# A two-layer hybrid decoder trunk on one core: early weight loads for blocked jobs, whole S5 table steps on one engine, memory through DRAM, and a new order of the work

## The chip, the cores and the metric

The kernel runs on one core of a Trainium2 chip. The metric is the device time of one execution in microseconds; of several runs the median is taken. The engines are TensorE (PE in the profile), VectorE (DVE), ScalarE (ACT), GpSimd (POOL) and SyncE (SP), which here issues every DMA.

## The reference, cut to what matters

The input is x of 512 tokens by 1024 channels in float32, 256 memory tokens, and weights for two layers. Each layer computes

```python
h = rms_norm(x, norm_pre)
c = h @ w_in                       # 9668 columns, split among the branches and the merge gates
y0 = rwkv7(c_A)                    # 4 heads, delta-rule state over the tokens
y1 = dsa(c_B, positions)           # an indexer keeps 128 keys per query, attention over these
y2 = retention(c_C, positions)     # chunks of 128 tokens
y3 = s5(c_D)                       # diagonal complex state space model, then a GLU
y4 = cross_attention(c_X, rms_norm(mem, norm_mem) @ w_mem_kv)
m  = sum(sigmoid(gate_i) * (y_i @ w_branch[i]) for i in range(5))
x  = x + rms_norm(m @ w_out, norm_post)
```

and the second layer starts from the x of the first.

## The kernel before, in words

The large products run on TensorE in three passes: each float32 operand is split into a high and a low part (fp32r), and high by high, high by low and low by high are summed. A weight block of 256 KB is loaded by SP into a tile `raw` (five buffers), ScalarE casts it to `wh`, and VectorE forms the rest `wl = raw - wh` (four buffers each). A class `Load` does this; `prefetch(upto)` issues loads up to five blocks ahead of the one in use and splits up to two ahead.

All instructions are issued in an order that the Python program works out while it builds the kernel. It has two kinds of work. **Dense jobs** (`Job`) are products with weights: column groups of w_in by name (`rq`, `rk`, `rv`, `w`, `wg`, `xq`, ...), the memory's keys and values (`mem`, `mem1`), the gates of branch i with its branch projection (`g0` to `g4`), and the output projection of each half of the tokens. `select()` takes the next dense job: the first in the list `ORDER` whose inputs are there and for whose kept result there is room. Room is counted in tiles of the pools c1, c2 and c4 (10, 14 and 16 tiles). A job for which there is no room is not taken, and its weights are not loaded; if none can be taken, `prefetch` has nothing to load.

**Lanes** (`Lane`) are the branches, the tables of S5 (`tab`), the splits of the memory (`ms0`, `ms1`), the start of a layer and its end (`finish_out`). Each is a generator that yields between its steps. At most `MAXL` lanes are active; they are started in the order of `LANES`, each when its inputs are there and there is room (`dsa>0` waits for y0 too, `s5>2` for y2, and so on). `run` takes a step of the first active lane whose last step has ended by the planner's own clocks at least 1 us ago (`EARLY`), unless the planner has VectorE or ScalarE more than `LAG` us behind TensorE; otherwise it issues the next piece of the dense job. So the dense work fills the time between the steps of the branches.

Each engine executes its instructions in the order of issue, and so does SP with the DMAs.

The parts that the change touches: `select` and `dense` (jobs), `s5_tables` (the lane `tab`), `mem_transposed` and `mem_split` (the normalised memory `memT`, two c4 tiles that are held under the owner `mem` until `ms1` is done), `out_jobs` and `finish_out` (the output projection and the sum with x), and the lists `ORDER` and `LANES`. In `s5_tables` a table of powers is built by doubling: for m = 1, 2, 4, ... 64, and for the real and the imaginary part, two products and their sum or difference on 8 x m columns. For each single instruction `any_` asks the planner which of VectorE and GpSimd is free sooner. After the last doubling, SP stores the table to DRAM (`s5tab`).

Of the kernel before, what the change touches and what calls it, by code (L numbers as in the profile page):

```python
# [222 lines left out]
def hybrid_kernel(ctx: ExitStack, tc: tile.TileContext, x, mem, positions, norm_pre, norm_post, norm_mem, w_in,  # L223
# [21 lines left out]
    def sb(name, shape, dt=F32, bufs=2, lane="c", big=False):  # L245
# [5 lines left out]
        if n == 4096 and dt == F32:  # L251
            return bp.tile(list(shape), dt, name=name, tag="mg", bufs=1)
# [204 lines left out]
    def mem_transposed():  # L457
# [118 lines left out]
    class Job:  # L576


        def __init__(self, gen, loads, need=(), done=None, keep=None, frees=(), after=None, merge=None, gate=None):
            self.gen, self.loads, self.need, self.done, self.frees, self.after = gen, loads, need, done, frees, after  # L580
            self.owner, self.room = (keep[0], {keep[1]: keep[2]}) if keep else (None, {})
            self.taken, self.merge, self.gate = False, merge, gate
            jobs.append(self)

    taken, merging, queue, active, opened = [], [], [], [], []

    def select():
# [13 lines left out]
        jb = next((j for j in left if (j.after is None or j.after.taken) and have(j.need) and fits(j, lanes)), None)  # L601
        if jb is None:
# [3 lines left out]
        hold(jb.owner, **jb.room)  # L606
        if last(jb):
            hold("mhl0", c4=4)
# [189 lines left out]

    def mem_split(l):

        h = [sb("mh", [128, 4, NMEM], F32R) for _ in range(2)]
# [602 lines left out]
    def s5_tables(l):  # L1404
# [11 lines left out]
        def any_(n_, name, *a, **kw):  # L1416
            e = V if sched.soonest(dve=n_ / 960, pool=n_ / 450) == "dve" else G
            getattr(e, name)(*a, **kw)
# [4 lines left out]
        while m < 128:  # L1423
# [42 lines left out]
        m_ = m1.rearrange("p b i c -> p i b c")  # L1466
        for i, (a, b) in enumerate(((0, 0), (1, 1), (1, 0), (0, 1))):
            any_(128, "tensor_tensor", m_[:, i], Bt[:, a], f_[b], op=OP.mult)
        any_(128, "tensor_tensor", Bb[:, 0], m_[:, 0], m_[:, 1], op=OP.subtract)
        any_(128, "tensor_tensor", Bb[:, 1], m_[:, 2], m_[:, 3], op=OP.add)  # L1470
        yield

        def outer(dst, coef, mat, neg):

            for r_ in range(2):
                any_(1024, "memset", dst[r_], 0.0)

            def pr(a, b, d):
                any_(512, "tensor_tensor", d, coef[:, a, o, :, None].to_broadcast([128, nb, 4, 16]),
                     mat[:, b, :, None, :].to_broadcast([128, nb, 4, 16]), op=OP.mult)  # L1480
            for r_ in range(2):
# [3 lines left out]
                yield  # L1485
                if neg and r_:
                    any_(512, "tensor_scalar", m1, m1, -1.0, None, op0=OP.mult)
                for q in range(2):
                    h = slice(64 * q, 64 * q + 64)
                    any_(512, "tensor_tensor", dst[r_][h, :, :, q, :], m1[h], m2[h],  # L1490
                         op=OP.add if r_ and not neg else OP.subtract)
# [195 lines left out]
    def out_jobs(l):  # L1687
# [3 lines left out]
        for half in range(2):  # L1691
            lds = {(e, k): Load(wv[:, k:k + 2, 256 * e:256 * e + 256]) for e in range(4) for k in range(0, 8, 2)}

            def gen(half=half, lds=lds):
# [4 lines left out]
                g = ST[l, "npost"]  # L1699
                for e in range(4):  # L1700
                    o = slice(256 * (e % 2), 256 * (e % 2) + 256)
                    for k in range(8):
                        w = lds[e, k - k % 2]
                        if k % 2 == 0:
                            prefetch(w.idx)
                            if k == 2:
                                flush()
                        mh, ml = ST["mhl", l, half, k // 4]
                        for i in range(2):
                            if k == 0 and e % 2 == 0:  # L1710
                                pss[i][e // 2] = psb() if half == 0 or (i == 0 and e == 0) else psd()
                            t = slice(128 * i, 128 * i + 128)
                            p = pss[i][e // 2][:, o]
                            for a, (x_, y_) in enumerate(((mh, w.hi), (mh, w.lo), (ml, w.hi))):
                                T.matmul(p, x_[:, k % 4, t], y_[:, k % 2, :], start=k == 0 and a == 0 and e % 2 == 0,
                                         stop=k == 7 and a == 2 and e % 2 == 1, skip_group_check=True)
# [4 lines left out]
                    if e:  # L1721
                        a, b = (0, 512) if e == 1 else (256 * e, 256)
                        for i in range(2):
                            v = pss[i][a // 512][:, a % 512:a % 512 + b]
                            j = sched.ring("gth", 2, bp.tile([128, S], F32, name="gth", tag="gth", bufs=2))
                            A.activation(j[:, :b], v, AF.Square, scale=1.0 / 32, accum_out=rr[i][:, e - 1:e])
                            V.tensor_tensor(u[i][:, a:a + b], v, g[:, a:a + b], op=OP.mult)
                ST[l, "fin", half] = (u, rr, xi)
# [22 lines left out]
    def dense():  # L1751
        while True:
# [10 lines left out]
            prefetch(jb.loads[0].idx)  # L1763
# [178 lines left out]
```

## Time and profile before

| | |
|---|---|
| median of 3 runs | 1466.64 us (1465.48 to 1467.06) |
| the profiled execution | 1470.27 us, of which its span 1468.5 us |
| TensorE busy | 1394.2 us, 95% of the span, 7774 matmuls |
| VectorE, ScalarE, GpSimd busy | 942.5, 558.0 and 274.2 us |
| mean granted clock of TensorE | 0.971 |
| DMA | 168.51 MB, a mean of 115 GB/s |

The span runs from the first to the last instruction. TensorE's clock has two levels, 2.4 GHz (granted clock 1.0) and 1.2 GHz (0.5); the granted clock of a stretch is a mean over it. All instructions carry line 209, the line of the helper that records them, so that they are told apart by their tiles: `wh`, `wl` and `raw` are weights, `hh` and `hl` the normalised x, `mgs` the merged sum, `sar`, `sta` and `sem` the S5 tables, `dsc` the scores of DSA, `dac` its indexer, `xp` the cross-attention's probabilities, `ors` and `ou` the end of a layer.

### The profile page before, as it was taken

What the parts mean: (1) busy time and instruction counts of PE and PEld (TensorE: products, weight loads), DVE (VectorE), ACT (ScalarE), POOL (GpSimd) and SP (SyncE); (2) the same over time, 40 slices, a digit from 0 to 9 for tenths busy, and PEclk for the clock granted to TensorE, in tenths of its full rate; (3) what the DMA queues carried; (4) which work ended last, traced back from release to release, by engine and by line L of the source; (5) the groups of instructions that cost most, each with busy time, mean ns of one, the idle gap of its engine ahead of it and who ended that gap; (6) DMA issues with size and microseconds to landing.
All of it is one profiled execution on the core that took longest, in us unless ns stands there. A gap on an engine that the chain in (4) does not pass through costs nothing.

```text
span 1468.5 us, 21717 instructions
## 1 busy us (share of the span) xinstructions
PE 1394.2 (95%) x7774; PEld 1160.9 (79%) x7774; DVE 942.5 (64%) x2020; ACT 558.0 (38%) x1196; POOL 274.2 (19%) x336
## 2 busy tenths in 40 slices
PE   5998999999999999989986999999999999999997
PEld 5977678878888978768886987777888878877887
DVE  5776555657765977634664566577888777734555
ACT  4533443333333333333544452433332333243343
POOL 0365230000310121100008533220011101311000
PEclk9999889999999999979998999999999999999999
DMA  6741334355322533313564743234444323423355
GB/s 188 191 122 56 114 108 102 83 169 151 94 65 72 145 89 98 102 35 93 159 194 130 204 119 93 66 100 123 116 129 143 102 68 76 109 64 79 100 159 179
DMA packets 242839, 168.51 MB, mean 115 GB/s; under 512 B 27593, under 2 KB 228267, under 8 KB 242731
## 3 DMA queue, kind: packets, MB, share of 16 engines
q1 hardware_dynamic: 242731, 167.12, 41.1%
q8 instruction: 61, 1.00, 0.3%
q14 instruction: 47, 0.39, 0.1%
HBM read 143.49 MB, written 17.83 MB: 110 GB/s over the span
## 4 chain that ended last, share of the span: by engine, by line
PE 79%; DVE 6%; POOL 5%; DMA 4%; ACT 3%; issue 2%; SPq 1%; DVEq 0%; ACTq 0%; POOLq 0%
PE d L209 60%; PE b L209 19%; POOL sar L209 2%; DMA raw<-in_w_out_dram 1%; DVE wl L209 1%; SPq L209 1%; DMA raw<-in_w_in_dram 1%; POOL sm L209 1%; POOL sta L209 1%; DVE x L209 1%; POOL rsw L209 1%; ACT wh L209 0%; DMA npre<-in_norm_pre_dram 0%; DMA posi<-in_positions_dram 0%; POOL sem L209 0%
## 5 line engine op out<-in xcount | busy, mean ns | idle before, releaser
L209 PE MATMUL d<-hh,wh 128*128 128x512 f32 (+1 forms) x1232 | 489.8, 398 | 13.4 <-ACT wh L209 13.4
L209 PE MATMUL d<-hh,wl 128*128 128x512 f32 (+1 forms) x1232 | 475.6, 386 | 14.2 <-DVE wl L209 14.1
L209 PE MATMUL d<-hl,wh 128*128 128x512 f32 (+1 forms) x1232 | 473.9, 385 | 0.0
L209 DVE TENSOR_TENSOR wl<-raw,wh 128x512 fp32r<-128x512 f32 (+1 forms) x448 | 328.5, 748 | 120.5 <-ACT wh L209 118.5
L209 ACT CAST wh<-raw 128x512 fp32r<-128x512 f32 (+1 forms) x448 | 267.4, 618 | 127.2 <-PE d L209 74.1
L209 PEld LDWEIGHTS d<-hh,wh 128*128 128x128 f32 x1232 | 236.9, 192 | 73.7 <-ACT wh L209 15.6
L209 PEld LDWEIGHTS d<-hh,wl 128*128 128x128 f32 x1232 | 236.2, 192 | 66.4 <-DVE wl L209 18.4
L209 PEld LDWEIGHTS d<-hl,wh 128*128 128x128 f32 x1232 | 236.8, 192 | 42.5 <-issue 0.5
L209 POOL TENSOR_TENSOR mg<-mg,gth 128x512 f32<-128x512 f32 x48 | 67.9, 1415 | 459.7 <-DVE gth L209 459.7
L209 ACT ACTIVATE gth<-d 128x512 f32<-128x512 f32 (+1 forms) x90 | 52.0, 578 | 163.5 <-PE d L209 162.6
L209 DVE SCALAR_TENSOR_TENSOR gth<-gth,d 128x512 f32<-128x512 f32 x64 | 44.0, 687 | 102.9 <-PE d L209 97.5
L209 PE MATMUL b<-wh,mgs 128*128 128x256 f32 x320 | 63.7, 284 | 5.2 <-ACT wh L209 3.8
L209 PE MATMUL d<-yh,wh 128*128 128x512 f32 x160 | 63.3, 395 | 0.0
L209 PE MATMUL d<-yl,wh 128*128 128x512 f32 x160 | 63.2, 395 | 0.0
L209 PE MATMUL d<-yh,wl 128*128 128x512 f32 x160 | 63.2, 395 | 0.0
L209 PEld LDWEIGHTS b<-wh,mgs 128*128 128x128 f32 x320 | 52.2, 191 | 6.1 <-ACT wh L209 4.0
L209 DVE MAX8 dm<-dac 128x8 f32<-128x256 f32 (+2 forms) x96 | 53.0, 552 | 0.1
L209 DVE MATCH_REPLACE8 dac<-dm,dac 128x256 f32<-128x256 f32 (+2 forms) x96 | 52.1, 543 | 0.0
L209 POOL TENSOR_TENSOR ors<-ors,mhalf 128x1 f32<-128x1 f32 x8 | 4.6, 586 | 230.5 <-DVE ors L209 230.5
L209 PE MATMUL b<-wl,mgs 128*128 128x256 f32 x160 | 45.6, 285 | 0.6 <-DVE wl L209 0.6
L209 PE MATMUL d<-wh,mgs 128*128 128x256 f32 x192 | 41.3, 288 | 2.3 <-DVE ou L209 2.3
L209 POOL TENSOR_TENSOR rsw<-rsw,sinT 128x1024 f32<-128x1024 f32 (+1 forms) x12 | 28.9, 2412 | 67.2 <-DMA rsw<-rk 23.7
(397 smaller groups left out, 2084.4 us busy)
## 6 DMA issues: line engine op xcount, KB each, us to landing
raw<-in_w_in_dram SPq DMA_DIRECT2D x324, 256.0 KB, 3.3
raw<-in_w_out_dram SPq DMA_DIRECT2D x64, 256.0 KB, 3.1
raw<-in_w_branch_dram SPq DMA_DIRECT2D x40, 256.0 KB, 3.6
x<-in_x_dram SPq DMA_DIRECT2D x8, 512.0 KB, 6.1
raw<-in_w_mem_kv_dram SPq DMA_DIRECT2D x16, 256.0 KB, 2.7
s5tab<-sar SPq DMA_DIRECT2D x8, 256.0 KB, 2.4
s5Wi<-sar SPq DMA_DIRECT2D x4, 512.0 KB, 2.9
nn<-wNt SPq DMA_DIRECT2D x8, 256.0 KB, 2.1
```

The source lines that it names most:

```text
L209: r = f(*args, **kw)
```

## The change

1. `select` may take a job for which there is no room: it is marked as not granted, its weights are loaded and split as for any job, and `dense` grants it (and only then issues its matmuls) when room has come free. Only one such job is open at a time, and none is taken while an active lane waits for something that is not there.
2. In `s5_tables` each group of instructions that follow from one another (two products and their sum) goes to one engine, chosen once for the group by `free_for`; the clearing of the outer products is always on GpSimd, and there is one more yield after each squaring of the factor.
3. The normalised memory is written to DRAM by the setup, its two tiles are given up after `ms0`, and `ms1` loads them again (and asks for 6 c4 tiles in place of 4).
4. In the last quarter of the output columns of the last two token tiles of layer 1, the two tiles are done one after the other, and the first is finished while the second is computed.
5. `LAG` goes from 7.5 to 11.5, `MAXL` from 4 to 6, and `ORDER` and `LANES` are new.

```diff
-LAG = 7.5
+LAG = 11.5
-MAXL = 4
+MAXL = 6
-ORDER = ("rv w rsg xq xsg ssg g4 g1 wg su mem di g2 dq dsg dk mem1 dv g3 g0",
-         "dv xsg w g3 di rsg su wg ssg g2 g4 dk g0 dq dsg g1")
-LANES = ("rwkv ms0 tab dsa>0 s5 ret ms1>3 x idx", "x ret idx tab s5>2 rwkv dsa")
+ORDER = ("rsg rv w wg g0 xq xsg di su dsg ssg dq g4 g2 dk mem1 dv g3 mem g1",
+         "xsg dq g0 w di rsg wg g4 su dsg ssg dk dv g3 g1 g2")
+LANES = ("ret idx>4 s5>4 ms1>3 rwkv dsa ms0 tab x>2", "idx>4 dsa>0 tab ret x rwkv>t s5")
...
+        for k in range(2):
+            SY.dma_start(memd[k], memT[k])
...
-        jb = next((j for j in left if (j.after is None or j.after.taken) and have(j.need) and fits(j, lanes)), None)
-        if jb is None:
+        if any(not t.granted for t in begun):
+            return False
+        able = [j for j in left if (j.after is None or j.after.taken) and have(j.need)
+                and not (opened and j.gate is not None and j.gate[1] == 0)]
+        jb = next((j for j in able if fits(j, lanes)), None)
+        if jb is None and able:
+            jb = able[0]
+            if last(jb) or not all(have(q.need) for q in active):
+                return False
+            jb.granted = False
+        elif jb is None:
             jb = left[0]
             if not fits(jb, lanes) and (active or not fits(jb)):
                 return False
...
             for r_ in range(2):
-                any_(nb * m, "tensor_tensor", d[r_], a[0], e[r_], op=OP.mult)
-                any_(nb * m, "tensor_tensor", t, a[1], e[1 - r_], op=OP.mult)
-                any_(nb * m, "tensor_tensor", d[r_], d[r_], t, op=OP.add if r_ else OP.subtract)
+                en = free_for(3 * nb * m)
+                en.tensor_tensor(d[r_], a[0], e[r_], op=OP.mult)
+                en.tensor_tensor(t, a[1], e[1 - r_], op=OP.mult)
+                en.tensor_tensor(d[r_], d[r_], t, op=OP.add if r_ else OP.subtract)
                 yield
             m *= 2
             if m < 128:
                 cmul(G, em2, em, em, ea, eb)
                 em, em2 = em2, em
+                yield
...
+                    if e == 3 and half and l == L - 1:
+                        for i in range(2):
+                            for k in range(8):
+                                if i == 0 and k % 2 == 0:
+                                    prefetch(lds[e, k].idx)
+                                products(e, k, i)
+                                if k % 2:
+                                    yield
+                            evict(e, i)
+                            if i == 0:
+                                flag(f"out{l}1a")
+                        continue
...
             prefetch(jb.loads[0].idx)
+            while not jb.granted:
+                if room_for({"c4": 6} if jb.last else jb.room):
+                    grant(jb)
+                else:
+                    yield 1e9
...
-                    "ms1": Lane(lambda: mem_split(1), ("ms0",), "ms1", c4=4),
+                    "ms1": Lane(lambda: mem_split(1), ("ms0",), "ms1", c4=6),
```

## Rows read from the trace of the kernel before

**Rows 1.** The page's first part: busy time, share of the span, instructions.
```profile
PE 1394.2 (95%) x7774; PEld 1160.9 (79%) x7774; DVE 942.5 (64%) x2020; ACT 558.0 (38%) x1196; POOL 274.2 (19%) x336
```

**Rows 2.** Windows: stretch, length, each engine's busy time, granted clock, DMA share, GB/s.
```profile
0.00:45.00 45.00, 28.70 (x190) 26.67 (x191) 27.41 (x61) 23.63 (x43) 2.51 (x10) 0.96 0.64 183
...
103.00:245.00 142.00, 130.29 (x717) 105.51 (x717) 82.58 (x188) 59.70 (x148) 43.10 (x43) 0.90 0.36 102
245.00:620.00 375.00, 373.67 (x1977) 304.46 (x1976) 261.05 (x560) 126.14 (x253) 48.86 (x37) 1.00 0.39 104
620.00:670.00 50.00, 44.13 (x210) 35.47 (x209) 15.56 (x38) 17.61 (x41) 2.78 (x2) 0.80 0.24 64
...
735.00:905.00 170.00, 147.64 (x1057) 136.28 (x1056) 100.49 (x185) 75.68 (x184) 73.75 (x115) 0.93 0.54 155
905.00:1421.00 516.00, 513.28 (x2651) 413.39 (x2651) 346.16 (x746) 182.30 (x367) 66.37 (x55) 1.00 0.37 100
1421.00:1469.00 48.00, 37.10 (x306) 36.09 (x304) 29.22 (x59) 20.77 (x54) 2.28 (x4) 0.94 0.53 172
```

**Rows 3.** Waits of TensorE over the span: total us, times, longest us.
```profile
PE d L209 <- DVE wl L209: 15.4, 7, 11.3
PE d L209 <- ACT wh L209: 13.4, 7, 6.2
```

**Rows 4.** Timeline of VectorE, 793 to 812 us: start, length, instruction, idle before it.
```profile
807.99 0.69 DVE L209 TENSOR_TENSOR sar<-sar,sta 128x512 f32<-128x512 f32 x1 [13.63 <-POOL sta L209]
808.60 2.49 DVE L209 TENSOR_TENSOR wl<-raw,wh 128x512 fp32r<-128x512 f32 x4
```

**Rows 5.** Timeline of GpSimd, 797 to 810 us.
```profile
806.91 1.04 POOL L209 TENSOR_TENSOR sta<-sar,sem 128x512 f32<-128x512 f32 x1
```

**Rows 6.** Windows around the stall in the S5 tables of layer 1.
```profile
797.70:809.30 11.60, 0.33 (x3) 0.12 (x2) 1.31 (x3) 1.62 (x3) 10.02 (x18) 0.63 0.12 46
809.30:814.50 5.20, 5.16 (x24) 5.16 (x25) 1.79 (x3) 0.06 (x1) 0.78 (x3) 0.50 0.65 146
814.50:822.00 7.50, 7.35 (x61) 7.11 (x61) 4.09 (x4) 4.50 (x10) 7.42 (x10) 1.00 1.06 269
```

**Rows 7.** Waits of the DMA queue, 784 to 822 us: total, times, longest.
```profile
SPq L209 <- POOL sar L209: 11.8, 1, 11.8
```

**Rows 8.** Timeline of the DMA queue, 793 to 813 us.
```profile
805.98 3.52 SPq L209 DMA_DIRECT2D s5tab<-sar  x4
...
812.40 0.57 SPq L209 DMA_DIRECT2D raw<-in_w_in_dram  x1
```

**Rows 9.** Tile wl, 784 to 890 us: ns min/median/max, first and last start.
```profile
L209 DVE TENSOR_TENSOR wl<-raw,wh x35: 678/693/1784, 784.1 to 885.9; 128x512 fp32r<-128x512 f32 x35
```

**Rows 10.** Timeline of the DMA queue, 125 to 150 us.
```profile
134.71 9.07 SPq L209 DMA_DIRECT2D kv<-gth  x2
...
145.07 2.94 SPq L209 DMA_DIRECT2D raw<-in_w_in_dram  x5
```

**Rows 11.** Windows of 10 us.
```profile
190.00:200.00 10.00, 8.72 (x60) 7.59 (x59) 6.20 (x10) 4.81 (x15) 9.05 (x10) 0.83 0.01 2
200.00:210.00 10.00, 8.34 (x43) 6.50 (x45) 2.80 (x7) 4.13 (x16) 1.78 (x2) 0.50 0.92 273
```

**Rows 12.** Tile xp in layer 0: ns min/median/max, first and last start, forms.
```profile
L209 ACT ACTIVATE xp<-b,xmx x16: 464/473/480, 193.4 to 230.8; 128x256 f32<-128x256 f32 x16
```

**Rows 13.** Tile dac in layer 0.
```profile
L209 DVE TENSOR_SCALAR dac<-b,diw x3: 478/618/750, 403.2 to 540.6; 128x256 f32<-128x256 f32 x1, 128x384 f32<-128x384 f32 x1, 128x512 f32<-128x512 f32 x1
```

**Rows 14.** Tile dsc in layer 0.
```profile
L209 ACT ACTIVATE dsc<-dsc,dmx x16: 386/556/721, 530.5 to 643.6; 128x128 f32<-128x128 f32 x4, 128x256 f32<-128x256 f32 x4, 128x384 f32<-128x384 f32 x4, 128x512 f32<-128x512 f32 x4
```

**Rows 15.** Timeline of the end, 1459.9 to 1469 us.
```profile
1460.79 0.38 ACT L209 ACTIVATE gth<-d 128x256 f32<-128x256 f32 x1
...
1462.12 1.06 POOL L209 TENSOR_TENSOR ors<-ors,mhalf 128x1 f32<-128x1 f32 x2 [22.85 <-DVE ors L209]
1462.70 2.74 DVE L209 SCALAR_TENSOR_TENSOR x<-ou,ors,x 128x512 f32<-128x512 f32 x4 [0.46 <-POOL ors L209]
```

More of the change, by code (lines that the diff above doesn't have):

```diff
@@ L251, in sb @@
         if n == 4096 and dt == F32:
-            return bp.tile(list(shape), dt, name=name, tag="mg", bufs=1)
+            return sched.ring("mg", 1, bp.tile(list(shape), dt, name=name, tag="mg", bufs=1))
         c, w = next((c, w) for c, w in ((1, 256), (2, 516), (4, 1032), (16, 4096)) if n <= w and not (big and c == 1))
@@ L581, in __init__, with grant @@
             self.owner, self.room = (keep[0], {keep[1]: keep[2]}) if keep else (None, {})
-            self.taken, self.merge, self.gate = False, merge, gate
+            self.taken, self.merge, self.gate, self.granted = False, merge, gate, True
             jobs.append(self)
-    taken, merging, queue, active, opened = [], [], [], [], []
+    taken, merging, queue, active, opened, begun = [], [], [], [], [], []
+    def grant(jb):
+        hold(jb.owner, **jb.room)
+        if jb.last:
+            hold("mhl0", c4=4)
+        jb.granted = True
     def select():
@@ L605, in select @@
                 return False
-        hold(jb.owner, **jb.room)
-        if last(jb):
-            hold("mhl0", c4=4)
+        jb.last = last(jb)
+        begun[:] = [t for t in begun if not t.granted] + [jb]
+        if jb.granted:
+            grant(jb)
         if jb.merge is not None:
@@ L796, in to_fm @@
         return ps
+    memd = dp.tile([2, 128, 4, NMEM], F32, name="memd")
     def mem_split(l):
+        if l:
+            memT[:] = [sb("memT", [128, 4, NMEM]) for _ in range(2)]
+            for k in range(2):
+                SY.dma_start(memT[k], memd[k])
+            yield
         h = [sb("mh", [128, 4, NMEM], F32R) for _ in range(2)]
@@ L1485, in outer @@
                 yield
+                en = free_for(1024)
                 if neg and r_:
[L1487 removed]
+                    en.tensor_scalar(m1, m1, -1.0, None, op0=OP.mult)
                 for q in range(2):
                     h = slice(64 * q, 64 * q + 64)
[L1490 to L1491 removed]
+                    en.tensor_tensor(dst[r_][h, :, :, q, :], m1[h], m2[h], op=OP.add if r_ and not neg else OP.subtract)
                     yield
@@ L1699, in gen, with products @@
                 g = ST[l, "npost"]
-                for e in range(4):
-                    o = slice(256 * (e % 2), 256 * (e % 2) + 256)
+                ST[l, "fin", half] = (u, rr, xi)
+                def products(e, k, i):
+                    mh, ml = ST["mhl", l, half, k // 4]
+                    w = lds[e, k - k % 2]
+                    o = slice(256 * (e % 2), 256 * (e % 2) + 256)
+                    if k == 0 and e % 2 == 0:
+                        pss[i][e // 2] = psb() if half == 0 or (i == 0 and e == 0) else psd()
+                    t = slice(128 * i, 128 * i + 128)
+                    p = pss[i][e // 2][:, o]
+                    for a, (x_, y_) in enumerate(((mh, w.hi), (mh, w.lo), (ml, w.hi))):
+                        T.matmul(p, x_[:, k % 4, t], y_[:, k % 2, :], start=k == 0 and a == 0 and e % 2 == 0,
+                                 stop=k == 7 and a == 2 and e % 2 == 1, skip_group_check=True)
@@ L1702, in gen @@
                     for k in range(8):
-                        w = lds[e, k - k % 2]
                         if k % 2 == 0:
-                            prefetch(w.idx)
+                            prefetch(lds[e, k].idx)
                             if k == 2:
                                 flush()
-                        mh, ml = ST["mhl", l, half, k // 4]
                         for i in range(2):
[L1710 to L1716, printed above, removed]
+                            products(e, k, i)
@@ L1721, in gen @@
                     if e:
-                        a, b = (0, 512) if e == 1 else (256 * e, 256)
                         for i in range(2):
[L1724 to L1728, printed above, removed]
+                            evict(e, i)
             after = Job(gen, list(lds.values()), done=f"out{l}{half}", need=tuple(f"merged{l}{i}" for i in range(5)),
@@ L1828, in run @@
                     hold("memkv" + pick.name[2], c4=4)
-                    if pick.name == f"ms{L - 1}":
-                        release("mem")
+                    release("mem")
                 if pick.name[0] == "y":
@@ L1906, in hybrid_kernel @@
         for i in range(4):
-            lanes += [Lane(lambda l=l, i=i: finish_out(l, i), (f"out{l}{i // 2}",), f"t{l + 1}{i}", c4=1)]
+            lanes += [Lane(lambda l=l, i=i: finish_out(l, i), (f"out{l}1a" if l == L - 1 and i == 2 else f"out{l}{i // 2}",),
+                           f"t{l + 1}{i}", c4=1)]
     run(lanes)
```

26 lines of the change are left out of this document (17 added, 9 removed).

## The prediction

> **What bounds the kernel now.** I read the page's busy times first: TensorE is busy for 1394.2 of 1468.5 us, far ahead of VectorE with 942.5 [rows 1]. The reader is to see that the time can only fall where TensorE stands still or runs at the lower clock; both are small, so a large edit can only move a little. Nothing is taken from TensorE's work itself.
>
> Next the windows, cut by stage [rows 2]. Length less busy time is the idle time; length times (1 less the granted clock) is what the lower clock costs at most.
>
> - 0 to 45 us, start: 45.0 - 28.7 = 16.3 idle.
> - 103 to 245 us, retention, RWKV and cross-attention of layer 0 begin: 11.7 idle, and 142 x 0.10 = 14.2 by the clock.
> - 245 to 620 us: 1.3 idle, clock 1.00.
> - 620 to 670 us, the end of DSA in layer 0: 5.9 idle, 50 x 0.20 = 10.0 by the clock.
> - 735 to 905 us, from layer 0 to layer 1: 22.4 idle, 170 x 0.07 = 11.9 by the clock.
> - 905 to 1421 us, the body of layer 1: 2.7 idle, clock 1.00.
> - 1421 to 1469 us, the end: 10.9 idle.
>
> So two long bodies leave some 4 us in 891, and the rest, about 70 us idle and some 36 by the clock, sits in five places. The change must be priced there. The waits then name what ends TensorE's longest single stops: 11.3 us for a `wl`, 6.2 us for a `wh` [rows 3].
>
> **S5 table steps on one engine.** The 11.3 us stop is in layer 1's tables. VectorE had been given the last difference of the table, whose product was given to GpSimd; it stood 13.63 us before it, and four splits `wl` were queued behind it [rows 4]. GpSimd reached that product only at 806.91 us, ending at 807.95 [rows 5]. TensorE waited, fell to the lower clock, and then worked 5.2 us at 0.50, which costs another 2.6 us [rows 6]. With the three instructions of a step on one engine VectorE can't stand there: at most 11.3 + 2.6 = 13.9 us come back.
>
> But what is late next? SP waited 11.8 us for the same table, before its store [rows 7]; the store went out at 805.98 and the next weights only at 812.40 [rows 8]. The four splits done in one run behind the stop are four blocks in hand; a block of 256 tokens is 12 matmuls, and 61 matmuls took 7.35 us at full clock, 0.12 each, so four blocks last 5.8 us [rows 4, 6]. If SP's wait kept its length, TensorE would stop some 6 us later for `raw` instead, and nothing would be won. The change also adds a yield after each of six squarings. A lane's next step waits 1 us beyond its modelled end and for the next piece of dense work, six matmuls or 0.72 us; six such yields move the store back by about 10 us in the order, close to the 11.8 it waits. What remains, about 2 us, is covered by the 5.8 in hand. Bounds 0 and 13.9; I take 11, near the upper one.
>
> A rule of the Trainium skill speaks against this part. In this stage a split `wl` has a median of 0.693 us and a longest of 1.784, so some take 1.1 us more than others [rows 9]. The Trainium skill, page "SBUF — State Buffer", section "Who interferes with whom", says that a VectorE instruction with two SBUF inputs and a GpSimd instruction that reads SBUF exclude one another for the whole instruction. By that rule steps that go wholly to GpSimd would hold up more splits; the longest split agrees with it, though the row does not name its cause.
>
> **Weights of a blocked job.** At 145.07 us five weight loads start at once, right behind two stores of the memory's keys and values that held SP from 134.71 to 143.78 [rows 10]; TensorE's 6.2 us stop for a `wh` follows from them [rows 3]. Loads taken earlier stand ahead of those stores, so that most of the stop goes: 4 us. From 190 to 200 us no weights move (2 GB/s), from 200 to 210 the DMA is at 0.92 and TensorE idle for 1.7 us at clock 0.50 [rows 11]; with the blocks there, dense work begins some us sooner: 1 us. For the rest of this stage the new order counts: six lanes in place of four, and two c4 tiles of the memory given up after `ms0`. I take 5 of the 20 us left. Bounds of the whole: 0 and 11.7 + 14.2 = 25.9; I take 10.
>
> **The end of layer 0.** The loss between 620 and 670 us is DSA's last steps with no dense work left: its exponentials run until 643.6 [rows 14]. They wait for the indexer, which began at 403.2 us [rows 13], though cross-attention was through its exponentials at 230.8 [rows 12]. The new lanes start the indexer behind cross-attention and no longer hold DSA back for RWKV, so both can begin up to 170 us sooner, and its gate work then stands beside other branches. Bounds 0 (another branch is last in its place) and 5.9 + 10.0 = 15.9; I take 10.
>
> **The last tiles in turn.** Behind the last matmul the two tiles share the chain: two evictions on ScalarE, the second 0.38 us, two powers on GpSimd in 1.06 us, four halves of the sum on VectorE in 2.74 us [rows 15]. With the first tile out of the way, half of the sum (1.37) and one eviction leave the chain, part of which overlapped already. Bounds 0.5 and 2; I take 1.4.
>
> **Memory through DRAM.** Two stores and two loads of 512 KB more, 2.1 MB in 168.5; the arithmetic stays. They wait in SP's queue for ScalarE's copies, with weight loads behind them. Nothing from below if blocks are in hand; from above a hold like that of the two stores, 9.07 us [rows 10]. They fall where no such stop of TensorE shows, so I take 0.5.
>
> **`LAG` and `MAXL`.** More lane instructions may stand in VectorE's and ScalarE's queues ahead of a split, which is the wait of [rows 3]. Below: nothing, since the two bodies leave 4 us with VectorE 67 to 70% busy [rows 2]. Above: the 4 us by which `LAG` grows, once in each of ten branch passes (five branches, two layers), 40 us. The bodies speak for the lower end; I take 4.
>
> **Sum.** 11 + 10 + 10 + 1.4 - 0.5 - 4 = 27.9 us. The profiled execution took 1470.27 us, its span 1468.5; this gives 1442.4. The median lies 3.6 us below that execution, so the forecast for a median is 1439 us, 1.9% faster. Some 0.2%, 3 us, is what a measurement of this kernel can tell from no change.
>
> **Rivals.**
> - *SP takes the stall over.* The store of the S5 table waits as long as before, with the weights behind it. For it: the 11.8 us [rows 7]. Against: the six yields. The 11 us are lost: 1450 us.
> - *Another end is left bare.* The new order in layer 0 only moves the hole of 620 to 670 us and leaves the early stage as it is: the 10 and the 5 us are lost, 1454 us, or, with a hole as large as the old one beside it (15.9), no change. For it: some branch is always last. Against: layer 1 already runs 516 us with 2.7 idle, by a different order [rows 2].
> - *GpSimd holds the splits.* More steps run on GpSimd, and one in six of the stage's 35 splits is held for 1.1 us on the path [rows 9]: 6.6 us, 1446 us. The page "SBUF — State Buffer" of the Trainium skill gives the rule. Against: the steps before the last difference were on GpSimd already [rows 5].
> - *The losses go altogether.* S5, the early stage and the end of layer 0 reach their upper bounds: 55.7 + 2 us, 1409 to 1413 us.
> - *Slower: lane work ahead of the splits.* With `LAG` at 11.5 the splits come up to 4 us later in each branch pass, 40 us in place of the 4 taken: 1475 us. It decides from eight passes of the ten that cost the full 4 us (1439 - 4 + 32 = 1467). For it: every long stop of TensorE now is a wait for a split [rows 3]. Against: up to two blocks are split ahead.
>
> **How the numbers follow.** Chances: forecast 0.48 (its own range 1427 to 1450), SP 0.12, another end 0.13, of which 0.04 no change, GpSimd 0.03, all losses gone 0.08, slower 0.16. Faster: 0.48 + 0.12 + 0.09 + 0.03 + 0.08 = 0.80; within 0.2%: 0.04; slower: 0.16. The range leaves out the slower case and half of no change: 1411 to 1466 us.
>
> **What would show it.** In the new profile no stop of TensorE above 5 us in the tables of layer 1, and VectorE not waiting for `sta`; SP's wait for `sar` below 6 us. Five-block bursts of weights ahead of, not behind, TensorE's stops in the first 250 us, and a granted clock of 0.95 there. No stretch of half clock before layer 0's output projection. The output's last sums half as long. Between 905 us and the end still under 8 us idle. The prediction is wrong if the two bodies show new idle time for `wl` or `wh`, or a branch of layer 0 or 1 ends after all dense work is used up.

## The result and the profile after

The changed kernel takes 1430.17 us, the median of 4 runs (1427.26 to 1431.76); the kernel before took 1466.85 (4 runs, 1465.48 to 1469.01). The ratio is 0.9746, with a 95% interval of 0.9726 to 0.9767: 2.5% faster, where 1.9% was forecast. The time lies inside the range and 9 us below the forecast of 1439. The profiled execution took 1431.76 us, its span 1430.0.

The page's first part, against [rows 1]:

```profile
PE 1373.7 (96%) x7774; PEld 1147.8 (80%) x7774; DVE 950.2 (66%) x2027; ACT 558.3 (39%) x1196; POOL 279.1 (20%) x329
```

TensorE has the same 7774 matmuls and is busy 20.5 us less. Its work is the same, so these microseconds are above all time that it no longer spends at the lower clock (mean granted clock 0.986 in place of 0.971). The other 18 of the 38.5 are idle time (74.3 before, 56.3 after).

The windows of [rows 2], here at the same times of the new span (stretch, length, busy time of TensorE, weight load, VectorE, ScalarE and GpSimd, granted clock, DMA share, GB/s):

```profile
103.00:245.00 142.00, 137.94 (x781) 111.80 (x780) 90.53 (x203) 66.19 (x161) 47.77 (x43) 0.95 0.41 117
245.00:620.00 375.00, 372.02 (x2025) 304.32 (x2024) 264.06 (x577) 130.13 (x269) 47.25 (x36) 1.00 0.38 104
620.00:670.00 50.00, 50.00 (x217) 40.41 (x216) 24.14 (x38) 16.84 (x31) 3.34 (x2) 1.00 0.40 111
...
905.00:1390.00 485.00, 481.58 (x2553) 391.00 (x2553) 334.55 (x686) 172.87 (x355) 63.46 (x47) 1.00 0.39 103
```

From 103 to 245 us the idle time is 4.1 us in place of 11.7 and the clock 0.95 in place of 0.90; from 620 to 670 us nothing is left of 5.9 idle and of a clock of 0.80. The two long bodies are nearly as full as before (3.0 us idle in the first in place of 1.3).

Equal times aren't equal work, though. A better cut is where the output projection of a layer begins, at its first cast of the merged sum (`mgs` on ScalarE, 664.9 and 1364.3 us before, 635.7 and 1326.6 after). Up to there the dense products are the same whatever their order. Windows of the kernel before, cut so:

```profile
0.00:664.90 664.90, 626.78 (x3382) 515.39 (x3383) 428.19 (x966) 249.07 (x528) 131.83 (x162) 0.96 0.40 110
664.90:1364.30 699.40, 673.58 (x3808) 561.91 (x3807) 457.04 (x951) 267.03 (x576) 140.12 (x170) 0.98 0.42 115
1364.30:1468.50 104.20, 93.81 (x588) 83.57 (x586) 57.27 (x105) 41.86 (x93) 2.28 (x4) 0.97 0.48 147
```

And of the changed kernel:

```profile
0.00:635.70 635.70, 610.68 (x3382) 504.40 (x3383) 429.04 (x969) 249.86 (x529) 134.67 (x159) 0.98 0.43 118
635.70:1326.60 690.90, 669.96 (x3808) 559.97 (x3807) 463.85 (x955) 266.42 (x575) 141.77 (x166) 0.99 0.43 116
1326.60:1430.00 103.40, 93.08 (x588) 83.41 (x586) 57.29 (x105) 42.03 (x93) 2.69 (x4) 0.98 0.49 148
```

The counts of matmuls agree to the last one: 3382, 3808 and 588. So the three lengths can be subtracted: layer 0 gives 29.2 us (13.1 idle, 16.1 busy at the lower clock), layer 1 up to its output projection 8.5, the end 0.8.

The longest stops of TensorE, against [rows 3] (total us, times, longest us):

```profile
PE d L209 <- ACT wh L209: 13.5, 4, 8.4
...
PE d L209 <- DVE wl L209: 7.2, 7, 2.2
```

The 11.3 us stop for a `wl` is gone, and a stop of 8.4 us for a `wh` is new. It sits in the same place, layer 1's S5 tables. TensorE, VectorE and SP's queue there, in that order (start, length, instruction, idle before it and its releaser; for the DMA queue the length is until the data landed):

```profile
791.97 0.58 PE L209 MATMUL d<-hh,wh 128*128 128x256 f32 x1 [8.35 <-ACT wh L209]
```

```profile
791.95 0.69 DVE L209 TENSOR_TENSOR wl<-raw,wh 128x512 fp32r<-128x512 f32 x1 [10.12 <-ACT wh L209]
```

```profile
771.05 3.10 SPq L209 DMA_DIRECT2D raw<-in_w_in_dram  x3
779.86 5.05 SPq L209 DMA_DIRECT2D s5tab<-sar  x4
784.96 1.40 SPq L209 DMA_DIRECT2D sBt<-in_s_b_re_dram  x2
786.40 1.31 SPq L209 DMA_DIRECT2D sBt<-in_s_b_im_dram  x2
787.81 2.66 SPq L209 DMA_DIRECT2D raw<-in_w_in_dram  x5
```

VectorE no longer waits for `sta` [rows 4]; it waits for weights. These stand in SP's queue behind the table's store, whose last part needs the difference that GpSimd ends at 784.09. No weight is loaded from 774.15 to 787.81 us, 13.7 us (18.3 before, 794.15 to 812.40). The forecast named this as a rival: SP takes the stall over. What it costs beside the stop, by two windows:

```profile
783.60:791.97 8.37, 0.02 (x2) 0.00 (x1) 0.02 (x1) 0.67 (x2) 3.34 (x8) 0.75 0.67 170
791.97:798.10 6.13, 6.13 (x27) 5.90 (x28) 4.10 (x5) 2.87 (x6) 2.49 (x3) 0.50 1.05 307
```

8.35 us idle and 6.13 us at half clock, half of it lost: 11.4 us, where the kernel before lost 13.9 at this place [rows 6].

### The profile page after: what moved, and what is told of

Read it like the earlier page. It is cut to its first block, busy times and chain, and to the rows that moved or that the text cites. A ratio compares the mean times of both kernels' runs of the same rounds, so it can differ in the third digit from the quotient of the medians.

```text
span 1430.0 us, 21718 instructions
## 1 busy us (share of the span) xinstructions
PE 1373.7 (96%) x7774; PEld 1147.8 (80%) x7774; DVE 950.2 (66%) x2027; ACT 558.3 (39%) x1196; POOL 279.1 (20%) x329
## 3 DMA queue, kind: packets, MB, share of 16 engines
q1 hardware_dynamic: 243307, 169.22, 42.6%
## 4 chain that ended last, share of the span: by engine, by line
PE 82%; DVE 6%; POOL 4%; DMA 3%; ACT 2%; issue 2%; SPq 1%; POOLq 0%; DVEq 0%; ACTq 0%
PE d L209 62%; PE b L209 19%; DVE wl L209 2%; POOL sar L209 2%; DMA raw<-in_w_out_dram 1%; POOL sta L209 1%; DMA raw<-in_w_in_dram 1%; DVE x L209 1%; SPq L209 1%; ACT wh L209 0%; DMA posi<-in_positions_dram 0%; DMA x<-in_x_dram 0%; DMA rsw<-rq 0%; POOL sem L209 0%; POOL rsw L209 0%
## 5 line engine op out<-in xcount | busy, mean ns | idle before, releaser
L209 PE MATMUL d<-hh,wh 128*128 128x512 f32 (+2 forms) x1232 | 488.3, 396 | 13.5 <-ACT wh L209 13.5
L209 PE MATMUL d<-hh,wl 128*128 128x512 f32 (+2 forms) x1232 | 474.3, 385 | 6.6 <-DVE wl L209 6.5
L209 PE MATMUL d<-hl,wh 128*128 128x512 f32 (+2 forms) x1232 | 472.1, 383 | 0.0
L209 DVE TENSOR_TENSOR wl<-raw,wh 128x512 fp32r<-128x512 f32 x448 | 334.0, 761 | 139.2 <-ACT wh L209 135.6
L209 ACT CAST wh<-raw 128x512 fp32r<-128x512 f32 x448 | 268.7, 617 | 165.6 <-PE d L209 111.9
L209 PEld LDWEIGHTS d<-hh,wh 128*128 128x128 f32 (+1 forms) x1232 | 235.6, 191 | 73.1 <-issue 15.0
L209 PEld LDWEIGHTS d<-hh,wl 128*128 128x128 f32 (+1 forms) x1232 | 234.8, 191 | 58.4 <-DVE wl L209 10.1
L209 PEld LDWEIGHTS d<-hl,wh 128*128 128x128 f32 (+1 forms) x1232 | 235.8, 191 | 42.3 <-issue 0.5
L209 DVE SCALAR_TENSOR_TENSOR gth<-gth,d 128x512 f32<-128x512 f32 x64 | 43.9, 686 | 107.2 <-PE d L209 103.4
```

The source lines that it names most:

```text
L209: r = f(*args, **kw)
```

## The experiments

Each run was timed beside runs of the kernel before on the same chip (its medians there 1466.55 to 1469.15). The last three columns are the profiled execution cut at the first `mgs` of each layer, as above; in every one of them TensorE's counts are 3382, 3808 and 588.

| run | median us | ratio to before, 95% | layer 0 | layer 1 | end |
|---|---|---|---|---|---|
| kernel before | 1466.85 | | 664.9 | 699.4 | 104.2 |
| changed kernel | 1430.17 | 0.9746 [0.9726, 0.9767] | 635.7 | 690.9 | 103.4 |
| e1, order, `LAG` and `MAXL` only | 1553.61 | 1.0586 [1.0557, 1.0615] | 731.7 | 717.2 | 103.9 |
| e2, all but these | 1475.70 | 1.0064 [1.0036, 1.0092] | 680.8 | 691.6 | 105.2 |
| e3, S5 stores on GpSimd's queue | 1422.30 | 0.9689 [0.9665, 0.9713] | 635.1 | 682.5 | 103.2 |
| e4, `select` of before | 1559.57 | 1.0622 [1.0581, 1.0663] | 733.6 | 713.5 | 102.7 |
| e5, no loads ahead | 1430.87 | 0.9756 [0.9718, 0.9795] | 629.2 | 693.3 | 102.8 |
| e6, loads after the grant | 1448.00 | 0.9871 [0.9834, 0.9908] | 647.6 | 693.0 | 103.4 |
| e7, memory held in SBUF | 1483.06 | 1.0107 [1.0075, 1.0139] | 687.9 | 690.3 | 103.7 |
| e8, e3 and x loaded later | 1425.14 | 0.9715 [0.9682, 0.9748] | 633.9 | 682.6 | 104.6 |
| e9, S5 steps as before | 1449.78 | 0.9868 [0.9842, 0.9895] | 646.3 | 700.7 | 103.9 |
| e10, last tiles together | 1428.75 | 0.9728 [0.9700, 0.9757] | 632.9 | 690.4 | 102.7 |
| e11, `LAG` 7.5 | 1436.68 | 0.9777 [0.9744, 0.9810] | 640.4 | 697.4 | 103.4 |
| e12, e5 and e3 | 1424.00 | 0.9699 [0.9672, 0.9725] | 631.3 | 686.6 | 103.3 |

The order is worked out for the whole program, so an edit undone in one place moves instructions elsewhere too. In e3 the order on TensorE, VectorE and ScalarE is that of the changed kernel to the last instruction, and in e10 that on TensorE, ScalarE and GpSimd; for the others the columns say where a difference lies.

### e1 and e2: the order alone, and all but the order

```diff
 # e1, on the kernel before (e2: the reverse, on the changed kernel)
-LAG = 7.5
+LAG = 11.5
-MAXL = 4
+MAXL = 6
-ORDER, LANES of the kernel before
+ORDER, LANES of the changed kernel
```

> The kernel before with the new ORDER, LANES, LAG and MAXL alone. If the order carries the gain of layer 0 (29 of the 38 us between the two traces), this lies at 1435 to 1445 us, and the first output projection starts near 636 us as in the changed kernel; what is missing is the S5 steps, the early loads and the end, about 3 to 10 us. If the new order needs the two c4 tiles and the early loads to be of use, it lies above 1455 us.

> The changed kernel with the old ORDER, LANES, LAG and MAXL. If the order carries the gain, this lies at 1453 to 1463 us (S5 2 to 3, end 1, early loads up to 6 us better than before) and the hole at the end of DSA in layer 0 stays. If the edits carry it, below 1445 us.

Neither half is faster. The new order by itself (with its `LAG` and `MAXL`) is 5.9% slower, the second of the cases expected; the edits without it are 0.6% slower, which neither case foresaw. In e1 SP's queue shows why (timeline, between them only the stores and loads of the branches):

```profile
164.79 0.53 SPq L209 DMA_DIRECT2D raw<-in_w_in_dram  x1
...
237.20 36.08 SPq L209 DMA_DIRECT2D wN<-nn  x4
273.33 0.97 SPq L209 DMA_DIRECT2D raw<-in_w_in_dram  x2
```

For 108 us not one weight is loaded: with these lanes no dense job finds room by the old rule (e4 and e5 below show that it is the rule), and the branches run alone. In that stretch TensorE is busy for less than half, at a granted clock of 0.57:

```profile
165.00:273.00 108.00, 49.65 (x260) 39.63 (x260) 55.23 (x135) 20.69 (x56) 19.26 (x16) 0.57 0.16 48
```

e2 keeps the old lanes. Its hole at the end of layer 0 is larger than before, from 619.2 to 673.8 us, with TensorE's longest stop (16.5 us) for DSA's exponentials `dsc`:

```profile
619.20:673.80 54.60, 35.43 (x140) 28.39 (x141) 21.74 (x60) 14.34 (x39) 0.00 (x0) 0.50 0.00 1
```

No weights move in it (1 GB/s): the dense work is used up, and DSA's last steps run alone. Its layer 1, though, takes 691.6 us against 699.4: what was won there doesn't need the new order.

### e4, e5 and e6: which part of `select` it is

e4 puts back the old `select`, in the changed kernel. e5 lets a job be taken when its own tiles are free, without the tiles that the old rule keeps back for the next lane, but opens no job ahead of its room. e6 opens jobs ahead as the change does, but loads their weights only when room is there.

```diff
 # e4
-        jb = next((j for j in able if fits(j, lanes)), None)
-        if jb is None and able:
-            jb = able[0]
-            ...
+        jb = next((j for j in left if ... and have(j.need) and fits(j, lanes)), None)
 # e5
-            if last(jb) or not all(have(q.need) for q in active):
+            if last(jb) or not all(have(q.need) for q in active) or not room_for(jb.room):
                 return False
-            jb.granted = False
 # e6 (`w.job` is set where a job is taken)
-        while lp["dma"] < min(len(stream), upto + NBUF["raw"]):
+        while lp["dma"] < min(len(stream), upto + NBUF["raw"]) and stream[lp["dma"]].job.granted:
```

> The changed kernel with the old select: a job without room is not taken and its weights not loaded. If early loads are worth what the forecast gave them, 4 to 5 us: about 1435 us, with a stop for wh of some 5 us in the first 250 us. If they hardly matter because the new order blocks seldom: 1428 to 1432 us. If the jobs come in another sequence through it, the time can go either way by more than 5 us, and the sequence of the gates tells it.

> The changed kernel, but a job is taken only when there is room for it at that moment, without the reserve for the next lane in the queue; no weights are loaded ahead for a job that must wait. The old select kept that reserve, and under the new order no weights moved for 108 and 119 us. Theory A (what the edit to select gives is that a job may use the room that was kept back for the next lane): 1430 to 1442 us, no gap in the weight loads above 40 us. Theory B (what it gives is the choice and the loads ahead of the room): near the 1559 us of the kernel with the old select, with a gap of 100 us.

> The changed kernel, but the weights of a job without room are loaded only once it has room; the choice of the job stays early. Theory A (the room, not the loads, matters): within 2 to 8 us of the changed kernel, 1432 to 1438 us, the loads alone being worth some 4 us each where TensorE stands ready. Theory B (early loads carry the gain): 1450 us or more, with stops of TensorE for wh of 5 us and more in the first 250 us.

e4 is as slow as e1, and its longest stop of TensorE is of the same kind, 42.6 us (e1: 40.1) which the profile puts down to `issue`, that is, to no wait that it shows; no weights are loaded for 118.7 us around it:

```profile
PE b L209 <- issue: 42.6, 1, 42.6
```

e5 takes as long as the changed kernel (0.9756 against 0.9746), as its theory A said, and its longest stretch without a weight load is 19.8 us. So with this order 129 us hang on `select`, and all of them come back without a single load ahead of a job's room: what counts is that a job may use the room which the old rule kept back for the next lane. The early loads matter in a narrower sense. In the change a job is committed before its room is there, and e6 shows what it would cost then to load late, 18 us by the medians; of the 14 between the two profiles 12 lie in layer 0. Neither theory had its 1448 us: A ended at 1438, B began at 1450. TensorE's waits in e6, against 13.5 us in 4 stops after the change, and SP's queue around the first long one, 6.85 us up to 156.58 (`kv<-gth` are the stores of the memory's keys and values):

```profile
PE d L209 <- ACT wh L209: 26.8, 9, 7.8
```

```profile
143.18 8.14 SPq L209 DMA_DIRECT2D kv<-gth  x2
...
152.59 2.73 SPq L209 DMA_DIRECT2D raw<-in_w_in_dram  x5
```

### e7: the memory's tiles

```diff
-        for k in range(2):
-            SY.dma_start(memd[k], memT[k])
 ...
-                    release("mem")
+                    if pick.name == f"ms{L - 1}":
+                        release("mem")
 ...
-                    "ms1": Lane(lambda: mem_split(1), ("ms0",), "ms1", c4=6),
+                    "ms1": Lane(lambda: mem_split(1), ("ms0",), "ms1", c4=4),
```

(The reloads in `ms1` go as well. `c4=4` and `c4=6` are the tiles that `ms1` asks for.)

> The changed kernel with the memory kept in its two c4 tiles until the second split, as before. If the two tiles decide where jobs and lanes of layer 0 find room, layer 0 ends later and this lies at 1440 to 1460 us, the difference ahead of the first output projection (636 us). If they hardly matter with the new select: 1427 to 1433 us.

The two c4 tiles are worth 53 us by the medians, nearly all of it in layer 0 (687.9 against 635.7); that is 23 us beyond the range expected. The early stage again runs dry, with no weights from 156.3 to 256.4 us:

```profile
103.00:245.00 142.00, 111.32 (x598) 90.06 (x596) 89.45 (x211) 51.68 (x131) 41.52 (x38) 0.77 0.28 82
```

### e9 and e3: the S5 tables

e9 puts back the choice of an engine for each instruction (the clearing of the outer products too) and takes out the extra yields. e3 is the changed kernel with the four stores of a layer's table issued by GpSimd, so that SP's queue no longer holds weights behind them.

```diff
 # e9
-                en = free_for(3 * nb * m)
-                en.tensor_tensor(...)   # three times
+                any_(nb * m, "tensor_tensor", ...)   # three times
 ...   (the same for the outer products)
                 em, em2 = em2, em
-                yield
 # e3
-                SY.dma_start(s5d["tab"][2 * l + b][:, r_], tab[r_][...])
+                to, of = s5d["tab"][2 * l + b][:, r_], tab[r_][...]
+                nc.gpsimd.dma_start(to, of)
+                sched.op("dma", "dma_start", (to, of), {})
```

> The changed kernel with the S5 tables as before: each instruction to the engine that the planner has free sooner, no yield after the squaring. If whole steps are worth what the forecast gave them (11 us): 1441 us. If the stop only moves between VectorE's queue and SP's (8.35 us of 11.3 are still there in the changed kernel): 1430 to 1434 us, with a stop of 8 to 12 us in the tables of layer 1 either way.

> The changed kernel with the four stores of each S5 table issued by GpSimd, right behind the instruction that ends the table, in place of SP; every engine's order is otherwise the same. If SP's wait for the table is what now stops TensorE at 792 us, the stop of 8.35 us and the half clock behind it (6.1 us at half, 3 us) go: 1418 to 1422 us. If GpSimd's own pace or the loads behind the store are the cause, the stop stays within 2 us: 1428 to 1431 us.

In e9 the pattern of [rows 4] is back: VectorE stands before the last difference, with four splits queued behind it, and TensorE stops 11.23 us for a `wl`. VectorE's timeline:

```profile
790.53 0.69 DVE L209 TENSOR_TENSOR sar<-sar,sta 128x512 f32<-128x512 f32 x1 [13.50 <-POOL sta L209]
791.14 2.49 DVE L209 TENSOR_TENSOR wl<-raw,wh 128x512 fp32r<-128x512 f32 x4
```

Layer 1 takes 9.8 us more than in the changed kernel, and layer 0 10.6; by the medians it is 19.6, more than either case expected. So the mechanism that was read from the profile before holds, and the edit is worth 9.8 us in layer 1, though a stop of 8.35 us stayed. What it does in layer 0 isn't traced.

e3 takes that one away. SP's queue in e3, where the changed kernel had the store of 5.05 us:

```profile
773.93 1.38 SPq L209 DMA_DIRECT2D sBt<-in_s_b_re_dram  x2
775.36 2.64 SPq L209 DMA_DIRECT2D sBt<-in_s_b_im_dram  x2
778.09 3.87 SPq L209 DMA_DIRECT2D raw<-in_w_in_dram  x5
```

The weights come at 778.09 in place of 787.81, TensorE has no stop above 1 us there, and layer 1 takes 682.5 us, 8.4 less (7.8 of them idle time), while layer 0 is the same within 0.6. The time is 1422.30 us against 1430.17: the fastest version, ahead of both kernels. Its cost on GpSimd's own engine is 2.25 us for the four issues:

```profile
784.10 2.25 POOL L1469 DMA_DIRECT2D s5tab<-sar  x4
```

### e8 and e12: on top of e3

e8 moves the loads of x for the output projection behind its first quarter, since they stand ahead of the weights when layer 0's projection ends. e12 is e3 with the `select` of e5.

```diff
 # e8
-                xi = [load_x(l, 2 * half + i) for i in range(2)]
+                xi = []
 ...
+                    if e == 1:
+                        xi.extend(load_x(l, 2 * half + i) for i in range(2))
```

> The kernel with the table's stores on GpSimd (1422 us), and the two loads of x in the output projection moved behind its first quarter of columns, so that they don't stand ahead of the weights of the second half. If those 1 MB are what makes the weights land late there (ScalarE waited 2.8 us for them, TensorE 3.7 us at 718 us), 2 to 4 us less in each layer at most: 1416 to 1420 us. If the wait comes from the instructions of the layer's end ahead of the casts, no change: 1420 to 1424 us.

> The two edits that were as good or better put together: a job is taken when there is room without the reserve (1431 us alone), and the table's stores go by GpSimd (1422 us alone). If the two are independent: 1420 to 1424 us, with no stop above 4 us behind the first 20 us. If loads ahead for a blocked job matter once the stop is gone: 1425 us or more.

In e8 the stop for `wh` at 715 us falls from 3.68 to 1.56 us, but a wait of 2.07 for S5's `sCg` appears, and the time doesn't fall (0.9715 against 0.9689, the intervals overlap; 1425.14 us is above both cases). e12 is the same as e3 (0.9699, 1424.00 us, as for independent edits), which shows once more that nothing measurable hangs on the loads ahead.

### e10: the last two tiles together

```diff
-                    if e == 3 and half and l == L - 1:
+                    if False:
 ...   (`finish_out` of the first tile waits for both tiles again)
```

> The changed kernel with the last two token tiles done together, as before; the order on TensorE, ScalarE, GpSimd and SP is the same by tile names. If the forecast's 1.4 us are right: 1431 to 1432 us, last matmul to end of the span 1 to 2 us longer. If the last DMA alone sets the end: within 0.5 us of 1430.

No difference can be measured (0.9728 against 0.9746; the 1428.75 us lie below both cases), and the end is 102.7 us long in place of 103.4. VectorE's last instructions after the change:

```profile
1422.20 0.42 DVE L209 TENSOR_TENSOR ou<-d,npost 128x256 f32<-128x256 f32 x1 [2.13 <-ACT gth L209]
1422.54 0.74 DVE L209 SCALAR_TENSOR_TENSOR x<-ou,ors,x 128x512 f32<-128x512 f32 x1
...
1423.47 0.75 DVE L209 SCALAR_TENSOR_TENSOR x<-ou,ors,x 128x512 f32<-128x512 f32 x1
1424.65 1.41 DVE L209 SCALAR_TENSOR_TENSOR x<-ou,ors,x 128x512 f32<-128x512 f32 x2 [0.44 <-POOL ors L209]
```

And in e10:

```profile
1419.98 2.74 DVE L209 SCALAR_TENSOR_TENSOR x<-ou,ors,x 128x512 f32<-128x512 f32 x4 [0.47 <-POOL ors L209]
```

The sums behind the last power take 1.41 us in place of 2.74, as planned. But the first tile's two halves, meant to run under the second tile's matmuls, stand in VectorE's queue behind a product of the second tile that waits 2.13 us for ScalarE's `gth`: they are done between that tile's instructions. One of them (0.74 us) holds up what leads to the last power; the other runs beside that power on GpSimd. From the last matmul to VectorE's last sum it is 4.41 us after the change, and 4.71 in e10 and in the kernel before: 0.3 us of the step came.

### e11: `LAG`

```diff
-LAG = 11.5
+LAG = 7.5
```

> The changed kernel with LAG at 7.5. If the larger LAG costs waits for splits (4 us by the forecast, 40 at most): 1390 to 1426 us. If it lets the branches' steps run sooner and the splits don't mind: 1432 to 1445 us. If neither: 1428 to 1432 us.

The smaller `LAG` isn't faster; the median is 6.5 us above the changed kernel's, but its runs spread from 1429.65 to 1442.99 and the intervals touch, so that whether it is slower stays open; it isn't faster, which the first case wanted. `MAXL` had no run: with 4 in place of 6 the planner gives the same instructions in the same order on every engine, so it does nothing.

## Why the prediction was right, and which of its steps were not

The direction, the places and the size of the whole were right. That the sum came within 9 us is in part luck: the S5 gain came only in small part from its place, and the early stage by another lever than the one priced. The terms, as far as the windows and runs show them:

| term | forecast us | measured us | from |
|---|---|---|---|
| S5 table steps | 11 | 8.5 | layer 1, 2.5 of it at the forecast place; e9: 9.8, and 10.6 in layer 0 |
| early stage, 103 to 245 us | 10 | 14.7 | idle 11.7 to 4.1, clock cost 14.2 to 7.1 |
| end of layer 0 | 10 | 15.9 | 620 to 670 us: nothing left of it |
| last tiles in turn | 1.4 | 0.3 | last matmul to last sum, 4.71 to 4.41; no difference in time by e10 |
| memory through DRAM | -0.5 | no stop seen | |
| `LAG` and `MAXL` | -4 | -1.7 at most | idle from 245 to 620 us: 1.3 to 3.0; `LAG` is not separated there |

The three terms from windows of layer 0 (early stage, body, end) are taken at equal times; they sum to 28.9 us, close to the 29.2 that the cut at equal work gives.

**S5.** The step on VectorE was right, and e9 shows it. So was the one on the yields. In us from the clearing of layer 1's table (at 771.75, 754.06 and 741.97):

| | before | e9 | changed |
|---|---|---|---|
| SP is through with the weights ahead of the store | 22.4 | 23.4 | 32.2 |
| the table's last difference ends | 36.9 | 37.2 | 42.1 |

SP comes to the store 9.8 us later, where about 10 were forecast. The step that failed is what is left of its wait, forecast at about 2 us and covered by four blocks in hand. SP waits in two parts, and the forecast counted only the first (11.8 us before, 1.9 more for VectorE's difference). And the table itself takes 5.2 us longer: 13.7 - 9.8 + 5.2 = 9.1.

```profile
SPq L209 <- POOL sar L209: 9.1, 2, 5.7
```

The stores and the four loads `sBt` between them and the weights, which the sum left out, take another 4.5 us. So for 13.7 us no weight is loaded, more than the blocks in hand cover. The table takes longer because VectorE no longer stands still beside it: GpSimd's instructions of the table are held up by 9.5 us in sum where they meet splits and other VectorE work, against 4.9 before (the last section shows which), and the last difference takes 1.28 us on GpSimd in place of 0.69 on VectorE.

So the rival "SP takes the stall over" was right of the place: of 13.9 us lost there 11.4 stayed. e3 shows the rival's mechanism; its price was 11 and is 8. Of the 8.5 us that layer 1 still gained, 2.5 come from this place and 1.7 from a stop of TensorE for `rk` at 886.7 us that the changed kernel doesn't have; the rest is shown by the sums of the window only.

**The end of layer 0.** Right, and the upper bound came: DSA's exponentials end at 566 us in place of 643.6 [rows 14], and dense work stands beside the branches until the output projection. They begin only 5 us sooner (525.9 us, before 530.5), but no longer wait in between: the indexer's last mask `dmk` is there at 512 us in place of 610. The first line is of the kernel before, the others of the changed one:

```profile
L209 DVE TENSOR_SCALAR dmk<-dac x3: 289/353/420, 472.0 to 609.7; 128x256 bf16<-128x256 f32 x1, 128x384 bf16<-128x384 f32 x1, 128x512 bf16<-128x512 f32 x1
```

```profile
L209 DVE TENSOR_SCALAR dmk<-dac x3: 288/364/423, 331.7 to 512.3; 128x256 bf16<-128x256 f32 x1, 128x384 bf16<-128x384 f32 x1, 128x512 bf16<-128x512 f32 x1
...
L209 ACT ACTIVATE dsc<-dsc,dmx x16: 385/556/723, 525.9 to 565.9; 128x128 f32<-128x128 f32 x4, 128x256 f32<-128x256 f32 x4, 128x384 f32<-128x384 f32 x4, 128x512 f32<-128x512 f32 x4
```

"Another end is left bare" didn't happen with the new lanes; with the old ones it did, in e2, to 54.6 us of half clock.

**The early stage.** The size was 4.7 us too small, and the working named the wrong lever, loads ahead of SP's stores and dense work a little sooner (5 of its 10 us). The stop behind the two stores of the memory's keys and values was read rightly: in e6, where weights wait for room, it is there again (6.85 us). But e5 has no such stop either, without any load ahead of a job's room, and e2, with loads ahead and the old order, keeps one of 5.1 us at this place. The room is worth far more: with the tiles kept back this order loses 129 us (e4), without the two of the memory 53 (e7); these two don't add. Six lanes in place of four, also named, did nothing. The forecast took the edits as terms of a sum; they are conditions of one another. e2 lacks the order, e4 the new `select`, e7 the memory's two tiles, e1 all but the order, and each is slower than the kernel before. The memory's way through DRAM, entered as a cost of 0.5, was one of the conditions.

**The slower rival.** That lane work ahead of the splits costs 40 us is refuted: the waits of TensorE's dense products for `wl` sum to 7.2 us, against 4.1 before without the stop in the S5 tables, and e11 isn't faster. (Its ground, that every long stop is a wait for a split, left out 10.2 us at the start, a wait for `xn`.)

**Its own signs.** VectorE doesn't wait for `sta`, the clock over the first 250 us is 0.96, and from 204 us to layer 0's output projection it is 1.00: as said. Half clock before that isn't gone altogether: 36.9 to 43.7, 159.8 to 170.0 and 200.7 to 204.1 us. No stop above 5 us in layer 1's tables, and SP's wait for `sar` below 6 us: false (8.35, and 9.1 in two parts). Bursts of five weights ahead of TensorE's stops: not as such, around the stores of the memory's keys and values two weights go between the stores and three behind them. The last sums are half as long behind the last power, but not in sum. That less than 8 us are idle from 905 us to the end was a slip, since the kernel before has 2.7 + 10.9 = 13.6 there [rows 2].

Open: which lane of the new order closes the hole in layer 0, since no run moves one lane alone; how e9 loses its 10.6 us in layer 0, where it has no single long stop; and whether whole table steps still matter once the stores go by GpSimd, since no run has the old steps with those stores.

## What to carry to other kernels

Cut a profile where the counted work is equal, and only then subtract: here three cuts with equal matmul counts split the gain into 29.2, 8.5 and 0.8 us. When a new order and new rules for buffers come together, price them together; each alone was slower, and the gain of layer 0 needed the new order and the room for dense work, but not its early loads. When a stall is taken from an engine, look at the DMA queue next: here a store that waited for data held all weights behind it, and another queue for that store gave 8 us. And look at what the engine, now busy, does to its neighbour: here the table took 5.2 us longer.

## What was not expected of the hardware

The table's stores land later from GpSimd's queue than from SP's, 5.3 us from issue in the median against 2.0, and yet the kernel is faster by 8 us, since no weight waits behind them. DMA issues in the changed kernel and in e3 (KB each, median us from issue to landing):

```profile
s5tab<-sar SPq DMA_DIRECT2D x8, 256.0 KB, 2.0
```

```profile
s5tab<-sar POOLq DMA_DIRECT2D x8, 256.0 KB, 5.3
```

GpSimd and VectorE instructions get longer beside each other, and by what VectorE reads. In the changed kernel GpSimd works at 69 instructions of layer 1's table. 34 of them overlap a split `wl` or a product `xn`, whose operands are all in SBUF (the memory that the engines work in): 21 of these are 0.1 to 1.1 us longer than the shortest of their form in the kernel before, 9.5 us in sum. 13 others overlap only `hl<-b,hh`, with `b` in PSUM (where TensorE leaves its results), and none of them is more than 0.01 us longer; nor are those that overlap nothing by more than 0.02. The same product of 128x128 beside two splits, and with VectorE idle:

```profile
764.77 1.72 DVE L209 TENSOR_TENSOR wl<-raw,wh 128x512 fp32r<-128x512 f32 x2 [0.24 <-ACT wh L209]
765.07 0.85 POOL L209 TENSOR_TENSOR sta<-sar,sem 128x128 f32<-128x128 f32 x1
...
767.13 0.40 POOL L209 TENSOR_TENSOR sta<-sar,sem 128x128 f32<-128x128 f32 x1
```

And one of 128x16 beside an `hl`, no longer than the 0.21 us of its form:

```profile
755.15 0.69 DVE L209 TENSOR_TENSOR hl<-b,hh 128x512 fp32r<-128x512 f32 x1 [0.17 <-ACT hh L209]
755.34 0.21 POOL L209 TENSOR_TENSOR sta<-sar,sem 128x16 f32<-128x16 f32 x1
```

VectorE pays too: it needs 4.37 us from 777.46 on for three splits of 0.69 each:

```profile
777.46 4.37 DVE L209 TENSOR_TENSOR wl<-raw,wh 128x512 fp32r<-128x512 f32 x3 [1.55 <-ACT wh L209]
```

The Trainium skill, page "SBUF — State Buffer", section "Who interferes with whom", says that the two exclude one another when VectorE reads two inputs from SBUF and GpSimd reads SBUF too. The trace agrees, by the 21 of 34 against none of 13. No stop of TensorE for a `wl` in this place exceeded 0.2 us, so the rival built on it cost nothing in the way that it was priced; but the table's end, for which SP's store and the weights behind it waited, came later by it.
